# Contrast adjustment on one core: rows of 48 KB in four buffers instead of rows of 32 KB in six

## The chip, the core and the metric

The kernel runs on one core of a Trainium2 chip (trn2). The metric is the device time in microseconds (us). Single runs are compared by their median. Where kernels are compared, a ratio is given: the mean time of one kernel's fast runs over that of the kernel before in the same rounds on the same chip, with a 95% interval. It is therefore not quite the ratio of the medians quoted beside it. The profile measures a span that is some 2 us shorter than the device time (237.3 for a run of 239.14).

## The reference

The input is 16 x 3 images of 512 x 512 floats, 50.3 MB. Each image is pulled away from its own mean and clipped:

```python
def reference(x, factor):                       # factor = 1.5
    mean = np.mean(x, axis=(2, 3), keepdims=True)
    return np.clip(mean + factor * (x - mean), 0, 1).astype(np.float32)
```

So each pixel is read once and written once, 100.7 MB in all, and an image's output needs its whole sum first: `clip(factor * x + (1 - factor) * mean)`.

## The kernel before

A tile is 128 rows of 8192 floats (32 KB a row, 4 MB), which is four whole images of 32 rows each. Twelve tiles go through a ring of six buffers and are changed in place. The vector engine (DVE) and the scalar engine (ACT) each sum a part of the row. Two matmuls with a block matrix of ones times `(1-factor)/n_pix` add up the rows of an image and leave the shift on each row. DVE scales, shifts and clips, and ACT's queue stores.

```python
P, ROW, BUFS, SHORT = 128, 8192, 6, 2048
FIRST = (SHORT, ROW - SHORT)          # tile 0 is stored in two pieces
SUM = 4352
# ... pools, block matrix
def compute(t):
    xt = ring[:, t % BUFS, :]
    own = sums[:, 2 * t : 2 * t + 2]
    nc.vector.tensor_reduce(out=own[:, 0:1], in_=xt[:, 0:SUM], ...)
    nc.scalar.activation(out=junk, in_=xt[:, SUM:ROW], func=Act.Copy, accum_out=own[:, 1:2])
    shift = bias[:, t : t + 1]
    nc.tensor.matmul(shift, blockw, own[:, 1:2], start=True, stop=False)
    nc.tensor.matmul(shift, blockw, own[:, 0:1], start=False, stop=True)
    # ... DVE: part = part * factor + shift; part = min(max(part, 0), 1)
    # ... store, on ACT's DMA queue
with tc.manual_schedule():
    load(0, c1=SHORT)
    load(0, c0=SHORT)
    load(1)
    load(2, n=2)                      # one DMA loads two tiles
    load(4, n=2)
    for t in range(n_tiles):
        compute(t)
        if t + BUFS < n_tiles:
            load(t + BUFS)            # waits until the store of tile t has landed
```

## Time and profile before

| | before |
|---|---|
| device time, median of 4 runs | 239.24 us (238.97 to 239.35) |
| span of the profiled run | 237.3 us |
| DMA, share of sixteen engines' span (loads + stores) | 49.7% + 49.2% |
| DVE busy, ACT busy | 69%, 18% |
| DMAs (loads + stores) | 11 + 13 |

The DMA engines are the resource to watch: they are busy all the time while DVE has a third of its time free. The prediction below shows the lines and how they are read.

### The profile page before, as it was taken

What the parts mean: (1) busy time and instruction counts of PE and PEld (TensorE: products, weight loads), DVE (VectorE), ACT (ScalarE), POOL (GpSimd) and SP (SyncE); (2) the same over time, 40 slices, a digit from 0 to 9 for tenths busy, and PEclk for the clock granted to TensorE, in tenths of its full rate; (3) what the DMA queues carried; (4) which work ended last, traced back from release to release, by engine and by line L of the source; (5) the groups of instructions that cost most, each with busy time, mean ns of one, the idle gap of its engine ahead of it and who ended that gap; (6) DMA issues with size and microseconds to landing.
All of it is one profiled execution on the core that took longest, in us unless ns stands there. A gap on an engine that the chain in (4) does not pass through costs nothing.

```text
span 237.3 us, 285 instructions
## 1 busy us (share of the span) xinstructions
PE 14.1 (6%) x48; PEld 12.0 (5%) x48; DVE 163.1 (69%) x38; ACT 43.2 (18%) x25; POOL 0.9 (0%) x9
## 2 busy tenths in 40 slices
PE   0010010001010001010010100100100100010000
PEld 0010010001010001010010100100100100010000
DVE  0079989048989328999989898891892795687000
ACT  2050230041050023050320504101400500500000
POOL 1000000000000000000000000000000000000000
DMA  7999999999999999999999999999999999999996
GB/s 297 410 442 442 421 442 359 456 439 441 442 436 414 403 431 442 442 442 442 436 442 436 414 409 425 442 442 442 442 436 442 436 420 403 425 442 442 442 442 265
DMA packets 3712, 100.66 MB, mean 424 GB/s; under 512 B 384, under 2 KB 384, under 8 KB 384
## 3 DMA queue, kind: packets, MB, share of 16 engines
q1 hardware_dynamic: 1840, 50.33, 49.7%
q10 hardware_dynamic: 1872, 50.33, 49.2%
HBM read 50.33 MB, written 50.33 MB: 424 GB/s over the span
## 4 chain that ended last, share of the span: by engine, by line
DMA 57%; DVE 29%; another core or an unknown queue 3%; PE 1%; SPq 1%; issue 0%; DVEq 0%
DMA ring<-in_x_dram 41%; DMA out_dram<-ring 16%; DVE sums L81 10%; DVE ring L91 9%; DVE ring L94 9%; PE bias L87 1%; SPq L76 1%; DVEq L91 0%
## 5 line engine op out<-in xcount | busy, mean ns | idle before, releaser
L81 DVE TENSOR_REDUCE sums<-ring 128x1 f32<-128x4352 f32 x12 | 56.2, 4683 | 45.7 <-DMA ring<-in_x_dram 45.7
L84 ACT ACTIVATE junk<-ring 128x3840 f32<-128x3840 f32 x12 | 40.8, 3403 | 163.3 <-DMA ring<-in_x_dram 107.5
L91 DVE TENSOR_SCALAR ring<-ring,bias 128x8192 f32<-128x8192 f32 (+2 forms) x13 | 54.1, 4163 | 8.9 <-PE bias L87 7.4
L94 DVE TENSOR_SCALAR ring<-ring 128x8192 f32<-128x8192 f32 (+2 forms) x13 | 53.3, 4099 | 0.4
L86 PE MATMUL bias<-sums,blockw 128*128 128x1 f32 x24 | 7.0, 361 | 190.8 <-ACT junk L84 190.8
L86 PEld LDWEIGHTS bias<-sums,blockw 128*128 128x128 f32 x24 | 6.0, 312 | 191.7 <-ACT junk L84 175.2
L87 PE MATMUL bias<-sums,blockw 128*128 128x1 f32 x24 | 7.0, 363 | 4.3 <-DVE sums L81 3.9
L87 PEld LDWEIGHTS bias<-sums,blockw 128*128 128x128 f32 x24 | 6.0, 311 | 5.3 <-DVE sums L81 5.0
L84 ACT ACTIVATION_READ_ACCUMULATOR junk<-ring 128x1 f32 x12 | 2.2, 186 | 0.0
L84 ACT ACT_TABLE_LOAD x1 | 1.3, 1283 | 0.7 <-PEq L129 0.7
L63 POOL MEMSET blockw<- 32x32 f32 x4 | 0.5, 117 | 0.2
L61 POOL MEMSET blockw<- 128x128 f32 x1 | 0.2, 204 | 0.3 <-POOLq L129 0.3
L129 POOL MEMSET const-bfloat16-1.0<- 128x1 bf16 x1 | 0.1, 111 | 0.0
L129 POOL MEMSET const-uint8-127<- 128x1 uint8 x1 | 0.1, 111 | 0.0
L129 POOL MEMSET const-float32-1.0<- 128x1 f32 x1 | 0.1, 108 | 0.0
L129 POOL MEMSET const-float32-0.0<- 128x1 f32 x1 | 0.1, 103 | 0.2 <-issue 0.2
## 6 DMA issues: line engine op xcount, KB each, us to landing
out_dram<-ring ACTq DMA_DIRECT2D x11, 4096.0 KB, 35.8
ring<-in_x_dram SPq DMA_DIRECT2D x7, 4096.0 KB, 49.7
ring<-in_x_dram SPq DMA_DIRECT2D x2, 8192.0 KB, 66.7
ring<-in_x_dram SPq DMA_DIRECT2D x1, 3072.0 KB, 11.7
out_dram<-ring ACTq DMA_DIRECT2D x1, 3072.0 KB, 28.2
ring<-in_x_dram SPq DMA_DIRECT2D x1, 1024.0 KB, 4.8
out_dram<-ring ACTq DMA_DIRECT2D x1, 1024.0 KB, 17.5
```

The source lines that it names most:

```text
L61: nc.gpsimd.memset(blockw, 0.0)
L63: nc.gpsimd.memset(blockw[a : a + ppi, a : a + ppi], wconst)
L76: nc.sync.dma_start(out=ring[:, b : b + n, c0:c1], in_=src)
L81: nc.vector.tensor_reduce(out=own[:, 0:1], in_=xt[:, 0:SUM], axis=mybir.AxisListType.X, op=Alu.add)
L84: nc.scalar.activation(out=junk, in_=xt[:, SUM:ROW], func=Act.Copy, accum_out=own[:, 1:2])
L86: nc.tensor.matmul(shift, blockw, own[:, 1:2], start=True, stop=False)
L87: nc.tensor.matmul(shift, blockw, own[:, 0:1], start=False, stop=True)
L91: nc.vector.tensor_scalar(out=part, in0=part, scalar1=factor, scalar2=shift, op0=Alu.mult, op1=Alu.add)
L94: nc.vector.tensor_scalar(out=part, in0=part, scalar1=0.0, scalar2=1.0, op0=Alu.max, op1=Alu.min)
L129: nc = _bacc.Bacc("TRN2", target_bir_lowering=False, num_devices=1)
```

## The change

The intent is fewer and longer transfers: rows of 48 KB, so that six images fill a tile of 6 MB and eight tiles do; sixteen DMAs in place of 24. A row of 12288 floats is three thirds of 4096, and an image is 64 thirds, so some rows hold parts of two images. Each row therefore gets five partial sums, which the GpSimd engine multiplies with class masks; one matmul gives totals for all classes, and DVE picks one shift for each third. ACT scales one or two thirds, DVE the rest and the clip. Cut to its core:

```diff
-ROW = 8192
-BUFS = 6
-SHORT = 2048
-FIRST = (SHORT, ROW - SHORT)
-SUM = 4352
+PART = 4096
+ROW = 3 * PART
+HALF = PART // 2
+BUFS = 4
+FIRST = (HALF, ROW - HALF)
+HEAD = (ROW,)
 ... masks and block matrix built on GpSimd
     def compute(t):
+        nc.vector.tensor_reduce(out=own[:, 0:3], in_=xt[:, 0 : 3 * HALF] as 3 x 2048, ...)
+        for m, a, b in (3, 3 * HALF, 4 * HALF), (4, 2 * PART, ROW):
+            nc.scalar.activation(out=part, in_=part, func=Act.Copy, accum_out=own[:, m : m + 1])
+        pool.tensor_tensor(out=spread[:, t, :], in0=own (broadcast), in1=cls, op=Alu.mult)
+        nc.tensor.matmul(totals[:, t, :], blockw, spread[:, t, :], start=True, stop=True)
+        nc.vector.tensor_tensor(out=picked[:, t], in0=totals (broadcast), in1=pick, op=Alu.mult)
+        nc.vector.tensor_reduce(out=bias[:, t, :], in_=picked[:, t], axis=X, op=Alu.add)
+        kd = 1 if 0 < t < n_tiles - 1 else 2
+        for k in range(kd, 3):          # ACT scales thirds kd..2, DVE those before
+            nc.scalar.activation(out=third, in_=third, func=Act.Identity, scale=factor,
+                                 bias=bias[:, t, k : k + 1])
 ... DVE clips the row, store
-        load(0, c1=SHORT)
-        load(0, c0=SHORT)
+        for n in HEAD: load(0, c, c + n)
         load(1)
         load(2, n=2)
-        load(4, n=2)
```

More of the change, by code (lines that the diff above doesn't have):

```diff
@@ L10 @@
 P = 128
-ROW = 8192
-BUFS = 6
-SHORT = 2048
-FIRST = (SHORT, ROW - SHORT)
-SUM = 4352
+PART = 4096
[4 more added lines that the diff above has]
+HEAD = (ROW,)
+IMGS = 6
+CLS = 3
+NSUM = 5
 @with_exitstack
@@ L32 @@
     Act = mybir.ActivationFunctionType
+    X = mybir.AxisListType.X
     B, C, H, W = x.shape
     n_img, n_pix = B * C, H * W
-    ppi = n_pix // ROW
-    per_tile = P // ppi
-    n_tiles = n_img // per_tile
-    assert ppi * ROW == n_pix and per_tile * n_tiles == n_img
+    n_tiles = n_img // IMGS
+    assert IMGS * n_pix == P * ROW and IMGS * n_tiles == n_img and n_pix % PART == 0
+    units = n_pix // PART
     factor = float(factor)
@@ L45 @@
     out_f = out.rearrange("b c h w -> (b c h w)")
-    def dram(ap, t, c0=0, c1=ROW):
-        return bass.AP(tensor=ap.tensor, offset=t * P * ROW + c0, ap=[[ROW, P], [1, c1 - c0]])
     consts = ctx.enter_context(tc.tile_pool(name="consts", bufs=1))
@@ L53 @@
     psum = ctx.enter_context(tc.tile_pool(name="psum", bufs=1, space=bass.MemoryType.PSUM))
-    sums = small.tile([P, 2 * n_tiles], f32, name="sums")
-    junk = small.tile([P, ROW - SUM], f32, name="junk")
-    bias = psum.tile([P, n_tiles], f32, name="bias")
-    blockw = consts.tile([P, P], f32, name="blockw")
-    nc.gpsimd.memset(blockw, 0.0)
-    for a in range(0, P, ppi):
-        nc.gpsimd.memset(blockw[a : a + ppi, a : a + ppi], wconst)
+    sums = small.tile([P, n_tiles, NSUM], f32, name="sums")
@@ new lines @@
+    spread = small.tile([P, n_tiles, CLS * NSUM], f32, name="spread")
+    picked = small.tile([P, n_tiles, 3, CLS * NSUM], f32, name="picked")
+    bias = small.tile([P, n_tiles, 3], f32, name="bias")
+    totals = psum.tile([P, n_tiles, CLS * NSUM], f32, name="totals")
+    pool = nc.gpsimd
+    of = consts.tile([P, IMGS, NSUM], f32, name="of")
+    pool.memset(of, 1.0)
+    step = [[-2 * units, IMGS], [1, NSUM]]
+    pool.affine_select(
+        out=of, in_=of, pattern=step, compare_op=Alu.is_ge, fill=0.0, base=0, channel_multiplier=6
+    )
@@ new lines @@
+    pool.affine_select(
+        out=of, in_=of, pattern=[[2 * units, IMGS], [-1, NSUM]], compare_op=Alu.is_gt, fill=0.0,
+        base=2 * units, channel_multiplier=-6,
+    )
+    cls = consts.tile([P, CLS, NSUM], f32, name="cls")
+    pool.tensor_tensor(out=cls, in0=of[:, 0:CLS], in1=of[:, CLS:IMGS], op=Alu.add)
+    pick = consts.tile([P, 3, CLS, NSUM], f32, name="pick")
+    for k in range(3):
+        pool.tensor_copy(
+            out=pick[:, k], in_=cls[:, :, 2 * k : 2 * k + 1].to_broadcast([P, CLS, NSUM])
+        )
@@ new lines @@
+    blockw = consts.tile([P, P], f32, name="blockw")
+    pool.memset(blockw, wconst)
+    period = CLS * units // 3
+    p0 = 0
+    while p0 < period:
+        first, last = 3 * p0 // units, (3 * p0 + 2) // units
+        p1 = p0 + 1
+        while p1 < period and (3 * p1 // units, (3 * p1 + 2) // units) == (first, last):
+            p1 += 1
+        cols = blockw.rearrange("q (h p) -> q h p", p=period)[:, :, p0:p1]
+        pool.affine_select(
+            out=cols, in_=cols, pattern=[[-3 * period, P // period], [0, p1 - p0]],
+            compare_op=Alu.is_ge, fill=0.0, base=2 - units * first, channel_multiplier=3,
+        )
+        pool.affine_select(
+            out=cols, in_=cols, pattern=[[3 * period, P // period], [0, p1 - p0]],
+            compare_op=Alu.is_gt, fill=0.0, base=units * (last + 1), channel_multiplier=-3,
+        )
+        p0 = p1
@@ L66, with dram @@
     ring = xpool.tile([P, BUFS, ROW], f32, name="ring")
-    def load(t, c0=0, c1=ROW, n=1):
-        b = t % BUFS
-        src = bass.AP(
-            tensor=x_f.tensor,
+    def dram(ap, t, c0, c1, n=1):
+        return bass.AP(
+            tensor=ap.tensor,
             offset=t * P * ROW + c0,
@@ L75, in load, with store @@
         )
-        nc.sync.dma_start(out=ring[:, b : b + n, c0:c1], in_=src)
+    def load(t, c0=0, c1=ROW, n=1):
+        b = t % BUFS
+        nc.sync.dma_start(out=ring[:, b : b + n, c0:c1], in_=dram(x_f, t, c0, c1, n))
+    def store(t, c0, c1):
+        b = t % BUFS
+        nc.scalar.dma_start(out=dram(out_f, t, c0, c1), in_=ring[:, b : b + 1, c0:c1])
     def compute(t):
         xt = ring[:, t % BUFS, :]
-        own = sums[:, 2 * t : 2 * t + 2]
+        own = sums[:, t, :]
         nc.vector.tensor_reduce(
-            out=own[:, 0:1], in_=xt[:, 0:SUM], axis=mybir.AxisListType.X, op=Alu.add
-        )
@@ L84, in compute @@
-        nc.scalar.activation(out=junk, in_=xt[:, SUM:ROW], func=Act.Copy, accum_out=own[:, 1:2])
-        shift = bias[:, t : t + 1]
-        nc.tensor.matmul(shift, blockw, own[:, 1:2], start=True, stop=False)
-        nc.tensor.matmul(shift, blockw, own[:, 0:1], start=False, stop=True)
+            out=own[:, 0:3], in_=xt[:, 0 : 3 * HALF].rearrange("p (m c) -> p m c", m=3), axis=X,
+            op=Alu.add,
+        )
+        for m, a, b in (3, 3 * HALF, 4 * HALF), (4, 2 * PART, ROW):
+            part = xt[:, a:b]
+            nc.scalar.activation(out=part, in_=part, func=Act.Copy, accum_out=own[:, m : m + 1])
@@ new lines, in compute @@
+        pool.tensor_tensor(
+            out=spread[:, t, :].rearrange("p (r m) -> p r m", r=CLS),
+            in0=own[:, None, :].to_broadcast([P, CLS, NSUM]),
+            in1=cls,
+            op=Alu.mult,
+        )
+        nc.tensor.matmul(totals[:, t, :], blockw, spread[:, t, :], start=True, stop=True)
+        nc.vector.tensor_tensor(
+            out=picked[:, t],
+            in0=totals[:, t, :][:, None, :].to_broadcast([P, 3, CLS * NSUM]),
+            in1=pick.rearrange("p k r m -> p k (r m)"),
+            op=Alu.mult,
+        )
@@ L88, in compute @@
+        nc.vector.tensor_reduce(out=bias[:, t, :], in_=picked[:, t], axis=X, op=Alu.add)
+        kd = 1 if 0 < t < n_tiles - 1 else 2
+        for k in range(kd, 3):
+            third = xt[:, k * PART : (k + 1) * PART]
+            nc.scalar.activation(
+                out=third, in_=third, func=Act.Identity, scale=factor, bias=bias[:, t, k : k + 1]
+            )
         c = 0
         for n in FIRST if t == 0 else [ROW]:
-            part = xt[:, c : c + n]
-            nc.vector.tensor_scalar(
-                out=part, in0=part, scalar1=factor, scalar2=shift, op0=Alu.mult, op1=Alu.add
-            )
+            end = c + n
+            for k in range(kd):
+                a, b = max(c, k * PART), min(end, (k + 1) * PART)
+                if a < b:
+                    part = xt[:, a:b]
+                    nc.vector.tensor_scalar(
+                        out=part, in0=part, scalar1=factor, scalar2=bias[:, t, k : k + 1],
+                        op0=Alu.mult, op1=Alu.add,
+                    )
+            part = xt[:, c:end]
@@ L96, in compute @@
             )
-            store(t, c, c + n)
-            c += n
-    def store(t, c0, c1):
-        nc.scalar.dma_start(out=dram(out_f, t, c0, c1), in_=ring[:, t % BUFS, c0:c1])
-    with tc.manual_schedule():
-        load(0, c1=SHORT)
-        load(0, c0=SHORT)
+            store(t, c, end)
+            c = end
+    with tc.manual_schedule():
+        c = 0
+        for n in HEAD:
+            load(0, c, c + n)
+            c += n
         load(1)
         load(2, n=2)
-        load(4, n=2)
         for t in range(n_tiles):
```

## The prediction

> **What bounds the kernel now.** I read the page's row of 40 slices first, then the DMA view of chosen stretches, then the timeline and the groups by shape. The DMA row asks whether the sixteen DMA engines ever rest:
>
> ```profile
> DMA  7999999999999999999999999999999999999996
> ```
>
> Only the first and last slice (5.9 us each) are below nine tenths. The DMA view of the stretch from 2 to 235 us says it exactly:
>
> ```profile
> DMA packets 3688, 100.60 MB, mean 432 GB/s; under 512 B 368, under 2 KB 368, under 8 KB 368
> q1 hardware_dynamic: 1832, 50.27, 50.4%
> q10 hardware_dynamic: 1856, 50.33, 50.1%
> ```
>
> q1 is the load queue, q10 the store queue. Together their packets take 100.5% of the sixteen engines' time: there is no hole to fill. So the time is first byte (1.75 us), packets, and the end. What a packet costs comes from the same view of two stretches. From 60 to 180 us every data packet is a row of 32 KB:
>
> ```profile
> DMA packets 1769, 52.20 MB, mean 435 GB/s; under 512 B 176, under 2 KB 176, under 8 KB 176
> q1 hardware_dynamic: 889, 26.51, 51.1%
> q10 hardware_dynamic: 880, 25.69, 49.6%
> ```
>
> Taking off the 176 tiny ones (semaphores), 1593 packets take 100.7% of 16 x 120 us = 1933 us, so 1.213 us each. From 26 to 34 us the first tile's short store (8 KB rows) runs beside a load:
>
> ```profile
> q1 hardware_dynamic: 82, 2.69, 78.3%
> q10 hardware_dynamic: 81, 0.66, 19.6%
> ```
>
> 81 packets in 19.6% of 128 us: 0.310 us each. The difference, 0.903 us for 24 KB, is 0.301 us per 8 KB, so a packet is about 0.009 us fixed plus 0.301 us per 8 KB. By this line 24 KB takes 0.912, 40 KB 1.514 and 48 KB 1.815 us. These are estimates.
>
> The chain of waits could mislead here:
>
> ```profile
> 116.30 37.73 DMA out_dram<-ring
> ...
> 154.17 49.57 DMA ring<-in_x_dram
> ...
> 203.76 4.70 DVE sums L81
> ```
>
> It puts 29% of the span on VectorE (DVE), yet while those DVE pieces ran the queues were full. What the compute may not do is leave the queues empty. In the timeline the reductions that start a tile (start, duration, then the wait before):
>
> ```profile
> 165.03 4.69 DVE L81 TENSOR_REDUCE sums<-ring 128x1 f32<-128x4352 f32 x1 [4.99 <-DMA ring<-in_x_dram]
> 184.40 4.68 DVE L81 TENSOR_REDUCE sums<-ring 128x1 f32<-128x4352 f32 x1 [4.99 <-DMA ring<-in_x_dram]
> 203.76 4.69 DVE L81 TENSOR_REDUCE sums<-ring 128x1 f32<-128x4352 f32 x1 [4.98 <-DMA ring<-in_x_dram]
> ```
>
> They come 19.37 us apart. A tile has 8 rows per DMA engine, so a load and a store side by side are 16 packets x 1.213 = 19.4 us. DVE waits 5 us of each such period for data. The unit costs of compute come from the groups by shape (busy us, mean ns):
>
> ```profile
> L81 DVE TENSOR_REDUCE sums<-ring 128x1 f32<-128x4352 f32 x12 | 56.2, 4683 | 45.7 <-DMA ring<-in_x_dram 45.7
> L94 DVE TENSOR_SCALAR ring<-ring 128x8192 f32<-128x8192 f32 x11 | 48.7, 4427 | 0.4
> L84 ACT ACTIVATE junk<-ring 128x3840 f32<-128x3840 f32 x12 | 40.8, 3403 | 163.3 <-DMA ring<-in_x_dram 107.5 <-DVE ring L94 55.8
> L91 DVE TENSOR_SCALAR ring<-ring,bias 128x6144 f32<-128x6144 f32 x1 | 3.4, 3418 | 0.0
> ```
>
> **What the Trainium skill says.** (1) "DMA: Bandwidth & Descriptors", section "Queues, rings and completion order": each DMA engine takes turns between the queues that have work, a whole packet at a time. The trace agrees: 82 load against 81 store packets between 26 and 34 us, though a load packet is three to four times as long. (2) "VectorE: DVE Perf Modes", "The perf-mode tier table": fp32 tensor_scalar runs at twice the rate of tensor_reduce. The trace agrees: 4683 ns for 4352 elements (4533 at 0.96 GHz plus 150) against 4427 for 8192 (4267 at two per cycle plus 160). (3) "ScalarE: Activation LUTs", "What ACT_TABLE_LOAD costs": 186 ns plus 0.833 ns per element, and about 93 ns more for each per-partition pointer operand. The trace has 3403 for 3840 elements, so 204 plus 3199; the pointer form isn't in it. (4) "GPSIMD Engine Reference", "Elementwise — side-by-side cycle accounting": 4497 ns for a two-input tensor_tensor of 2048 elements. No two-input GpSimd operation is in this trace; its memsets take 103 to 204 ns.
>
> **The change, part by part.**
>
> *Longer rows, fewer DMAs.* Before, per DMA engine: 16 packets of 8 KB, 16 of 24 KB and 176 of 32 KB, 4.96 + 14.59 + 213.49 = 233.0 us. After: the first store's 8 of 8 KB and 8 of 40 KB, then 56 + 64 rows of 48 KB, 2.48 + 12.11 + 217.80 = 232.4 us. That is 0.65 us less. Eight semaphore packets fewer at some 0.009 us are 0.07 us. The bytes stay.
>
> *The single first DMA.* The first packet leaves at the same 1.75 us. Tile 0 is complete only after 8 x 1.815 us, at about 16.3, and compute starts near 17.2 instead of 12.9. That costs nothing by itself: the loads of tiles 0 to 3 are queued at once and are 32 packets x 1.815 = 58 us of work for each DMA engine even without stores.
>
> *The new compute per tile.* The longest of DVE's sum, 6144/0.96 + 150 = 6.55 us, and ScalarE's (ACT) two, 204 + 1707 and 204 + 3413 with two accumulator reads of 186, 5.9 us. Then GpSimd's product of 15 numbers (estimate 0.2), the matmul pair (0.6 in the chain before), two tiny DVE operations (0.2 each, nearly all fixed cost) and four hand-overs of some 0.08: 1.55 us. Then ACT scales two thirds, 2 x (204 + 3413 + 93) less some overlap, 7.4 us with hand-over, beside DVE's one third of 4096 (2.36 us); DVE then clips 12288, 6400 + 160 = 6.56 us. Sum 22.1 us per tile. Next tile's sums start only then. The last tile gives DVE two thirds (4.7 us) and is 19.4 us.
>
> *Does the chain keep the queues full?* A load and a store of 48 KB rows side by side last 16 x 1.815 = 29.0 us, above 22.1. I walked the two queues packet by packet with these durations, about 0.4 us from last packet to consumer and 2.2 us from issue to first packet. The same walk on the kernel before gives a span of 236.8 where the trace has 237.3, and its loads land within about 1 us. For the changed kernel: tile 0 done at 37, tile 1 at 59, the double load lands at 75 (it shares the DMA engines with stores), tiles 2 to 6 done at 98, 120, 142, 164 and 186, the last load lands near 191, and the last store is issued at 211.6. Store 6 keeps the engines busy until 220. So no hole appears, with 6 us to spare at the end.
>
> *Sum.* 239.24 - 0.65 - 0.07 = 238.5 us, 0.3% less. I say 238.6, since I trust fixed packet costs more than the rest.
>
> **The rivals.** *Compute becomes the bound.* From the double load's landing, five tiles of 22.1 us run almost without pause on DVE and ACT in turn; ACT's in-order queue holds the next sums behind the store's issue. For it: three engines hand over inside one chain, and the GpSimd operation is unmeasured. Against it: DVE and ACT unit costs are from this trace. In the walk, 2 us more per tile changes nothing, 4 us more open a hole of 7 us before the last store and give 246 us, twice the ACT thirds 265. It needs more than 2.6 us of error in a sum where only about 0.5 is unmeasured. *Four big buffers starve the loads.* A load waits until a whole 6 MB store has landed, where before it was 4 MB and six buffers. That would show as a DMA hole near 105 to 135 us; the walk has the loads of tiles 4 to 7 queued 28 us before they land. If 2 us were lost at each of four re-uses, 246 us. *Longer packets are slower or faster per byte.* The fixed part could be larger than read off (a row split in two descriptors costs nothing much, 128 x 0.009 = 1.2 us). Then 239 to 240. *The gain is larger:* impossible beyond the first and last 2 us, since the bytes at the present rate already fill the span.
>
> **Range and chances.** The packet sum fixes the floor near 238; the small uncertainties are some tenths each way, with a tail above from the chain of compute: 237.6 to 240.3. Faster by over 2% would need 234.5, under the packet sum plus both ends: 1%. Slower by over 2% needs a hole of 5 us: 5%. Within 2%: 94%.
>
> **What would show it right or wrong.** In the profile after: DMA shares of the two queues that add up to about 100% between 2 and 235 us; 48 KB packets of 1.81 us; reductions in the steady part 22 us apart at first, DVE idle in each tile while ACT scales its thirds; the double load landing near 75; the last store issued near 211 to 214. Wrong if the DMA row shows slices under 9 anywhere but at the ends, most likely around 205 to 225 us, if a tile takes over 24.5 us on the compute engines, or if a 48 KB packet takes more than 1.82 us.

## The result, and the profile after

The changed kernel takes 241.82 us, the median of four runs (241.38 to 242.36), against 239.24 before. The ratio is 1.0111 (1.0083 to 1.0138). Two later sets of runs gave 1.0072 and 1.0113. It is a loss of about 1%, within the 2% that was given a chance of 94%, but outside the range of 237.6 to 240.3 and on the other side of the time before. The profiled run has a span of 239.3 us, so 2.0 us more than before.

The page's DMA row of 40 slices after:

```profile
DMA  7999999999999999999999999999999999999993
```

No slice between the ends fell under nine tenths, as predicted. The DMA view from 2 to 235 us shows the shares, and the same view from 60 to 180 us a part of the steady run:

```profile
q1 hardware_dynamic: 1124, 49.74, 50.0%
q10 hardware_dynamic: 1278, 50.23, 49.8%
...
DMA packets 1205, 52.20 MB, mean 435 GB/s; under 512 B 128, under 2 KB 128, under 8 KB 128
q10 hardware_dynamic: 633, 27.23, 52.4%
q1 hardware_dynamic: 572, 24.97, 48.3%
```

The DMA engines were as busy as before (99.8% against 100.5%). These views count a packet in the stretch in which it begins, so the bytes of a stretch are right only to about one packet for each engine (0.8 MB with rows of 48 KB). From 60 to 180 us both kernels moved 52.20 MB: in the steady part longer rows gained nothing that this view can show. The chain of waits runs over DVE and ACT for most of the first 121 us, then over a store, a load from 162.44 us and the last tile's sum. The last load was there for compute at 198.66 us, 7 us later than the walk had it (near 191). The reductions that start a tile, from the timeline:

```profile
121.22 6.54 DVE L129 TENSOR_REDUCE sums<-ring 128x3 f32<-128x6144 f32 x1
143.16 6.55 DVE L129 TENSOR_REDUCE sums<-ring 128x3 f32<-128x6144 f32 x1
169.67 6.55 DVE L129 TENSOR_REDUCE sums<-ring 128x3 f32<-128x6144 f32 x1 [4.46 <-DMA ring<-in_x_dram]
198.66 6.55 DVE L129 TENSOR_REDUCE sums<-ring 128x3 f32<-128x6144 f32 x1 [6.93 <-DMA ring<-in_x_dram]
```

While compute runs without a wait, tiles are 21.94 us apart; later they are 29.0 us apart and DVE waits for loads. The groups by shape (busy us, mean ns, then the idle time before):

```profile
L129 DVE TENSOR_REDUCE sums<-ring 128x3 f32<-128x6144 f32 x8 | 52.4, 6549 | 47.1 <-DMA ring<-in_x_dram 47.1
L155 ACT ACTIVATE ring<-ring,bias 128x4096 f32<-128x4096 f32 x14 | 51.3, 3702 | 18.3 <-DVE bias L149 18.3
L170 DVE TENSOR_SCALAR ring<-ring 128x12288 f32<-128x12288 f32 x7 | 45.9, 6560 | 30.4 <-ACT ring L155 30.3
L136 POOL TENSOR_TENSOR spread<-sums,cls 128x15 f32<-128x15 f32 x8 | 1.7, 212 | 199.9 <-DVE sums L129 199.9
```

The predicted costs were 6.55, 3.71, 6.56 and 0.2 us. Compute is as predicted; the loss is elsewhere.

**Where the 2.0 us are.** The view by stretches (stretch, its length, busy time of each engine, then clock, DMA share and GB/s) gives for the kernel before

```profile
46.00:56.00 10.00, 1.17 (x4) 1.00 (x4) 4.69 (x1) 3.50 (x2) 0.00 (x0) 1.00 1.00 433
...
110.00:190.00 80.00, 5.87 (x20) 5.01 (x20) 65.33 (x16) 17.48 (x10) 0.00 (x0) 1.00 1.00 433
```

and for the changed one

```profile
46.00:56.00 10.00, 0.00 (x0) 0.00 (x0) 4.92 (x3) 7.31 (x2) 0.00 (x0) 1.00 1.00 409
...
110.00:190.00 80.00, 1.83 (x6) 1.51 (x6) 52.28 (x16) 43.44 (x20) 0.64 (x3) 1.00 1.00 433
```

The last column matters. The same view gave 430 against 430 from 1.7 to 20 us, 418 against 422 from 20 to 46, and 436 against 434 from 56 to 110. Summed over the stretches up to 190 us, before has moved 81.25 MB and after 81.01. That is 0.24 MB, or 0.55 us at 433 GB/s. The dip from 46 to 56 us is where the second piece of tile 0 (rows of 40 KB) begins to be stored beside a load. The DMA share is 1.00 there: the engines don't rest, their packets take longer.

So the sixteen engines together are some 0.6 us late. One engine is much later, and that comes out only at the very end. Each of the sixteen DMA engines closes a transfer with one tiny packet (the semaphore), so the tiny packets in the DMA view of the last microseconds count the engines that have finished. Before, from 235.4 to 235.9 us and after that:

```profile
DMA packets 14, 0.00 MB, mean 0 GB/s; under 512 B 14, under 2 KB 14, under 8 KB 14
...
DMA packets 2, 0.00 MB, mean 0 GB/s; under 512 B 2, under 2 KB 2, under 8 KB 2
```

After, from 235.4 to 236.5, from 236.5 to 237.5, and from 237.5 us on:

```profile
DMA packets 14, 0.05 MB, mean 45 GB/s; under 512 B 13, under 2 KB 13, under 8 KB 13
...
DMA packets 2, 0.00 MB, mean 0 GB/s; under 512 B 2, under 2 KB 2, under 8 KB 2
...
DMA packets 1, 0.00 MB, mean 0 GB/s; under 512 B 1, under 2 KB 1, under 8 KB 1
```

Before, all sixteen finish within 0.58 us, the last at 236.05. After, thirteen finish by 236.5, and one only at 238.17 us. The kernel ends with its slowest engine, since each engine moves its own sixteenth. The trace doesn't name the engine of a packet, but a packet begins 0.003 to 0.004 us before the one ahead of it on its engine ends. Strung together so, the packets of the changed kernel make sixteen chains of 6 MiB each (one has a packet of 8 KB too many, another one too few). The Trainium skill has this for loads, in a note that it marks as unconfirmed: a bulk load "runs at the pace of its slowest engine" ("DMA: Bandwidth & Descriptors", section "iDMA fabric"). Here the last stores show it.

**Which packets took longer.** The chains show where each engine loses its time: how far its packets run over their usual duration (1.213 us for 32 KB, 1.815 for 48 KB), summed by the time at which they begin, in us.

| packets that begin | before, mean engine | after, mean engine | after, slowest engine |
|---|---|---|---|
| up to 8 us | 0.45 | 0.85 | 1.60 |
| 8 to 46 us | 0.81 | 0.40 | 0.29 |
| 46 to 56 us | 0.00 | 0.59 | 0.52 |
| 56 to 110 us | 0.00 | 0.28 | 0.85 |
| from 110 us | 0.01 | 0.06 | 0.35 |
| sum | 1.27 | 2.19 | 3.61 |

The mean end of the sixteen engines moved from 235.68 to 236.27 us. That is the 0.92 us of longer packets and 0.07 us of idle time, less about 0.4 us for fewer packets. The slowest engine also idled for 0.52 us just before its long packet at 82.9 us. So its lag was made at a few packets long before the end, and not in the last stores.

In the changed kernel 119 of the 1920 packets of 48 KB ran over by more than 0.03 us, all but one of them loads, and most of the time lost lies where a queue begins: at the first packets of all, where the store queue goes to its next DMA near 50 us, and on four engines where the load queue starts again after it has run dry. The DMA views from 1.7 to 2.8, from 48 to 52 and from 82.8 to 83.3 us have

```profile
q1 hardware_dynamic: 16, 0.79, 240.4%
...
q1 hardware_dynamic: 32, 1.57, 104.8%
...
q1 hardware_dynamic: 4, 0.20, 122.2%
```

The first number counts load packets, and the last is their time as a share of sixteen engines' stretch: 2.64, 2.10 and 2.44 us for each packet, where 1.815 is usual. In the kernel before, too, long packets lie at the first packets and where the store queue begins or goes to its next DMA (23 to 28 and 35 to 41 us), and nearly none come later.

### The profile page after: what moved, and what is told of

It is laid out like the page before. It is cut to its first block, busy times and chain, and to the rows that moved or that the text cites. A ratio compares the mean times of both kernels' runs of the same rounds, so it can differ in the third digit from the quotient of the medians.

```text
span 239.3 us, 247 instructions
## 1 busy us (share of the span) xinstructions
PE 4.9 (2%) x16; PEld 4.0 (2%) x16; DVE 131.4 (55%) x44; ACT 97.4 (41%) x47; POOL 5.0 (2%) x30
## 4 chain that ended last, share of the span: by engine, by line
DMA 40%; DVE 32%; ACT 8%; another core or an unknown queue 7%; issue 2%; PE 1%; POOL 0%; POOLq 0%; ACTq 0%; DVEq 0%; SPq 0%
DMA ring<-in_x_dram 22%; DMA out_dram<-ring 17%; DVE ring L170 14%; DVE sums L129 14%; ACT ring L155 8%; DVE ring L165 4%; PE totals L142 1%; DVE picked L143 0%; DVE bias L149 0%; POOL spread L136 0%; POOLq L217 0%; POOLq L136 0%; ACTq L155 0%; DVEq L170 0%
## 5 line engine op out<-in xcount | busy, mean ns | idle before, releaser
L135 ACT ACTIVATE ring<-ring 128x2048 f32<-128x2048 f32 (+1 forms) x16 | 44.1, 2754 | 94.1 <-DMA ring<-in_x_dram 64.7
L129 DVE TENSOR_REDUCE sums<-ring 128x3 f32<-128x6144 f32 x8 | 52.4, 6549 | 47.1 <-DMA ring<-in_x_dram 47.1
L170 DVE TENSOR_SCALAR ring<-ring 128x12288 f32<-128x12288 f32 (+2 forms) x9 | 52.6, 5849 | 30.5 <-ACT ring L155 30.3
L155 ACT ACTIVATE ring<-ring,bias 128x4096 f32<-128x4096 f32 x14 | 51.3, 3702 | 18.3 <-DVE bias L149 18.3
L165 DVE TENSOR_SCALAR ring<-ring,bias 128x4096 f32<-128x4096 f32 (+1 forms) x11 | 23.6, 2158 | 0.3
L142 PE MATMUL totals<-spread,blockw 128*128 128x15 f32 x16 | 4.9, 384 | 201.4 <-POOL spread L136 201.4
L142 PEld LDWEIGHTS totals<-spread,blockw 128*128 128x128 f32 x16 | 4.0, 311 | 202.1 <-POOL spread L136 202.1
L136 POOL TENSOR_TENSOR spread<-sums,cls 128x15 f32<-128x15 f32 x8 | 1.7, 212 | 199.9 <-DVE sums L129 199.9
L135 ACT ACTIVATION_READ_ACCUMULATOR ring<-ring 128x1 f32 x16 | 3.0, 186 | 0.0
L97 POOL TENSOR_SCALAR_AFFINE_SELECT blockw<-blockw 128x42 f32<-128x42 f32 (+2 forms) x5 | 0.9, 219 | 0.0
L101 POOL TENSOR_SCALAR_AFFINE_SELECT blockw<-blockw 128x42 f32<-128x42 f32 (+2 forms) x5 | 0.9, 218 | 0.0
```

Source lines behind the costliest of these rows:

```text
L97: pool.affine_select(out=cols, in_=cols, pattern=[[-3 * period, P // period], [0, p1 - p0]], compare_op=Alu.is_ge, fill=0.0, base=2 - unit ...
L101: pool.affine_select(out=cols, in_=cols, pattern=[[3 * period, P // period], [0, p1 - p0]], compare_op=Alu.is_gt, fill=0.0, base=units * ( ...
L129: nc.vector.tensor_reduce(out=own[:, 0:3], in_=xt[:, 0 : 3 * HALF].rearrange("p (m c) -> p m c", m=3), axis=X, op=Alu.add,)
L135: nc.scalar.activation(out=part, in_=part, func=Act.Copy, accum_out=own[:, m : m + 1])
L136: pool.tensor_tensor(out=spread[:, t, :].rearrange("p (r m) -> p r m", r=CLS), in0=own[:, None, :].to_broadcast([P, CLS, NSUM]), in1=cls, ...
L142: nc.tensor.matmul(totals[:, t, :], blockw, spread[:, t, :], start=True, stop=True)
```

## The experiments

Four theories are named in the texts written before the runs. **S**: the start of a DMA queue costs each engine a lag of its own, and more so with long packets. **Q**: the load queue of the changed kernel runs dry near 77 us (its view shows 90.9% store packets from 76 to 82 us) and restarting it costs. **T**, formed after the first runs: the ring of four is too tight, so queues have no reserve. **C**: the chain of compute issues the last store late. All ran with five rounds.

The engine-end spread below is the time between the first and the last of the sixteen closing packets of the last store, in the run's trace.

### The changed kernel unaltered, as a control

No edit.

> The changed kernel unaltered, as a control on the same chip as the next three. Its first runs spread from 241.38 to 242.36 us while the kernel before spread only from 238.97 to 239.35. Theory S (every start of a DMA queue costs each of the sixteen DMA engines a lag of its own, larger with 48 KB packets, and the slowest engine sets the end): 241.4 to 242.4 again, a ratio of 1.009 to 1.013, with one or two engines still storing up to 2 us after the others have ended. Theory C (the compute chain issues the last store late): the same time, but a stretch before the last store in which the DMA share falls below 0.95. Chance of the machine: a ratio near 1.000.

It took 240.53 us (240.22 to 242.92), ratio 1.0072 (1.0043 to 1.0102). Its engines ended between 235.52 and 237.30 us, a spread of 1.78. The loss is real, and so is its unsteadiness: the kernel before ranged from 239.02 to 239.65 in the same rounds.

### The first load split again

```diff
-HEAD = (ROW,)
+HEAD = (HALF, ROW - HALF)
```

> Only the first load is split again, 8 KB of each row first, then 40 KB. Theory S: the first packets, 2.4 to 3.4 us instead of 1.81 in the changed kernel, were the start-up lag; with 8 KB first packets the lag of the median engine at 6 us falls by about 0.3 us and that of the worst by up to 0.9, so 0.3 to 1.0 us faster than the control. Theory Q (the load queue runs dry from 77 to 82 us and restarting it costs) and theory C: no change beyond 0.2 us.

242.07 us (239.45 to 243.66), ratio 1.0073 (1.0037 to 1.0110): inconclusive. (The run of 243.66 us is slow and is left out of the ratio.) The runs spread over 4 us, and in the profiled one a single engine ended at 239.19, 2.5 us after the next. An effect of half a microsecond cannot be seen here.

### The first tile stored whole

```diff
-FIRST = (HALF, ROW - HALF)
+FIRST = (ROW,)
```

> Only the first tile's store is one DMA instead of 8 KB and 40 KB rows. It then alternates one to one with the loads, is issued near 37 us and lands near 70, before the double load lands near 75; so the load of tile 4 is queued before the load queue runs dry. Theory Q: the restart lag (mean 0.4 us, worst engine 1.4) goes, 0.4 to 1.5 us faster than the control, and no stretch of store packets alone near 77 to 82 us. Theory S without Q: the start of the store queue still costs its lag once, 0 to 0.3 us faster. Theory C: the first tile's store starts later, no gain or up to 0.5 us slower.

248.21 us, ratio 1.0383 (1.0362 to 1.0403). All three theories missed. The load of tile 4 was indeed queued in time, but the whole store took half of the DMA engines' time from 42 us on, so the double load landed at 83.6 instead of 76.9 us. Tile 2 then started at 84.0 and not at 77.3, the last store was issued at 224.6 and not at 218.1 us, and by 110 us the rate had fallen (421 GB/s from 56 to 110 us, where the changed kernel has 434). So filling that one gap didn't help. As the edit moved everything after it, it doesn't refute theory Q: in the changed kernel's own profile the first load packets after the gap are long on four engines, the slowest one among them.

### Packets of half the length

```diff
+        for a in range(c0, c1, ROW // 2):
+            e = min(a + ROW // 2, c1)
+            nc.sync.dma_start(out=ring[:, b : b + n, a:e], in_=dram(x_f, t, a, e, n))
 ... the stores likewise
```

> Each load and store moves the same tile as two DMAs of 24 KB rows; buffers and compute stay. If the length of a packet is what costs (theory S), first packets and restarts lose half as much: 0.5 to 1.2 us faster than the control. If the packets' fixed part of about 9 ns mattered as I predicted, 128 more packets on each engine would make it 1.1 us slower. Theory Q and C: within 0.3 us of the control.

240.92 us (240.43 to 242.47), ratio 1.0074, so the same as the control. The engines ended within 1.03 us of each other, less unevenly than the control's 1.78. The median engine ended later (236.55 against 235.98), the last one earlier (236.95 against 237.30). So S's gain did not appear, and of the predicted loss of 1.1 us the median engine shows about half. It is not a clean test of the packets' length: the first halves of tiles 2 and 3 are now loaded before their second halves, so that tile 2 starts at 59.0 us (77.3 in the changed kernel) and tile 3 at 105.7 (99.3).

### The kernel before with one whole first load

```diff
-        load(0, c1=SHORT)
-        load(0, c0=SHORT)
+        load(0)
```

> The kernel before, with only its first tile's load made one DMA of 32 KB rows. Theory S (long first packets make the start slower and uneven between the sixteen DMA engines): 0.3 to 0.9 us slower than the kernel before. Theory T (below: the tight ring, not the start, costs): within 0.2 us.

239.75 us (239.73 to 240.23), ratio 1.0030 (1.0017 to 1.0043). The one DMA for the first tile costs 0.6 us by itself where the ring is deep. The prediction had said that it costs nothing. Only some 0.3 us of this lie in the profiled span (237.54 us in the mean of the runs, 237.27 before); there the first packets run over by 0.70 us for each engine instead of 0.45. The rest lies outside the span, where no trace shows a cause.

### The kernel before with four buffers

```diff
-BUFS = 6
+BUFS = 4
-        load(4, n=2)
```

> The kernel before, with four buffers of 32 KB rows instead of six; packets, compute and first load stay. Theory T: what the change lost is depth of the ring. With six buffers the next loads lie queued long before the load queue needs them; with four a load is issued only as the queue runs dry, and each restart of a queue lengthens packets on some engines, which then never catch up. So 1 to 4 us slower than before, with engines ending up to 2 us apart. Theory S (length of packets, single first load): no change, within 0.3 us.

240.12 us (239.56 to 241.40), ratio 1.0044 (1.0025 to 1.0062). The view by stretches, the kernel before first, then this run:

```profile
56.00:76.00 20.00, 1.18 (x5) 1.00 (x4) 19.07 (x5) 3.50 (x2) 0.00 (x0) 1.00 1.02 439
...
56.00:76.00 20.00, 1.18 (x4) 1.00 (x4) 19.18 (x5) 3.50 (x2) 0.00 (x0) 1.00 1.00 418
```

The DMA engines are as full and move 21 GB/s less for 20 us, which is 0.96 us at 439 GB/s: nearly the whole loss. (The view is coarse, as the share of 1.02 shows; by the packets' own durations, load packets that begin between 66 and 68 us run over by 0.70 us for each engine.) From 110 to 190 us both have 433. In this stretch one store has landed and the next begins (66 to 68 us) beside a load. The engines end within 0.42 us, so the part of theory T about uneven ends isn't borne out here; its loss of rate is.

### The kernel before with the first tile stored whole

```diff
-FIRST = (SHORT, ROW - SHORT)
+FIRST = (ROW,)
```

> The kernel before, with the first tile stored by one DMA. In the changed kernel this same edit cost some 8 us, by theory T since its ring of four leaves the queues no reserve. Theory T: with six buffers it costs nothing, within 0.4 us of before. If the edit itself were bad (a later first store): several us slower here too.

241.36 us (241.16 to 241.56), ratio 1.0092 (1.0079 to 1.0105). T had said no cost. Fifteen engines ended by 236.1 us, before's own time, and one at 237.75: a spread of 2.23 with rows of 32 KB and six buffers. So a single slow DMA engine can set the end with short rows too, and a deep ring doesn't prevent it.

### The changed kernel with a shorter chain of compute

```diff
-        kd = 1 if 0 < t < n_tiles - 1 else 2
+        kd = 2
```

> The changed kernel with VectorE scaling two thirds of every tile, not of the first and last alone; a tile's chain of compute is then about 19.4 us instead of 22. Theory C (the chain of compute is the bound): 2 us or more faster than the control's 240.5. Theory T: stores can be queued a little earlier but a load still waits for the store of four tiles before, which is DMA time: within 0.7 us of 240.5, run-to-run spread of 2 us as before.

240.85 us (240.61 to 242.19), ratio 1.0080 (1.0063 to 1.0097). Tiles that don't wait are now 19.3 us apart instead of 21.9, and the last store is issued at 218.5 (218.1 before that edit), since the last load sets it. Theory C falls: 2.6 us less compute for each tile bring nothing.

### Both edits in the kernel before

```diff
-BUFS = 6
+BUFS = 4
-        load(0, c1=SHORT)
-        load(0, c0=SHORT)
+        load(0)
-        load(4, n=2)
```

> The kernel before, with both edits that cost alone: the first load whole (alone 1.0030) and four buffers (alone 1.0044). Neither changes the rows of 32 KB nor the compute. If the change's loss is its start and its tight ring, and long rows add nothing, the two add up: 1.0074, 240.9 us, which is the changed kernel's 1.0072 to 1.0111. If long rows themselves cost, this stays under 1.005.

240.08 us (239.68 to 240.84), ratio 1.0042 (1.0029 to 1.0055). The two don't add up: beside four buffers the whole first load costs nothing more. The changed kernel is at 1.0072 to 1.0113, so the rest, 0.3 to 0.7 percent of the time, must come from what these two edits don't have. The load packets near 68 us run over by 0.34 us for each engine here, half of what they do with four buffers alone, so the whole first load has shifted the meeting of the queues that costs. With these edits the engines end evenly: the DMA view from 236 to 237 us has all sixteen closing packets.

### The kernel before with five buffers

```diff
-BUFS = 6
+BUFS = 5
-        load(4, n=2)
+        load(4)
```

> The kernel before with five buffers of 32 KB rows. Theory T: the cost of a tight ring sets in when the load queue runs dry before the next store has landed; with five buffers the queued loads are 21 MB and the first store lands near 52 us, before they are through near 70, so no restart: within 0.2% of before, 239.1 to 239.6. If every buffer less costs in proportion: half of the 1.0 us that four buffers cost.

239.38 us (239.37 to 239.49), ratio 1.0010 (0.9998 to 1.0022). The cost sets in between five and four buffers, not in proportion, as T had it.

### The loads of tiles 2 and 3 apart

```diff
-        load(2, n=2)
+        load(2)
+        load(3)
```

> The changed kernel with the loads of tiles 2 and 3 as two DMAs, so that tile 2 is computed from about 60 us on and not from 77, and its store is queued some 17 us earlier. Theory T: the load of tile 4 still waits for the first store, near 77 us, so the load queue still runs dry once; but the store queue keeps a reserve. 0 to 0.7 us faster than the changed kernel's 240.5 to 241.8. Theory C (late compute): 1 us faster or more and the last store issued well before 218 us.

243.46 us (243.14 to 246.55), ratio 1.0202 (1.0165 to 1.0239): 2% slower, where every theory had a gain or nothing. Tile 2 did start at 59.8 us. The view by stretches, of the changed kernel first, then of this run:

```profile
56.00:76.00 20.00, 0.00 (x0) 0.00 (x0) 4.11 (x1) 0.00 (x0) 0.00 (x0) 1.00 1.00 434
76.00:92.00 16.00, 0.61 (x2) 0.50 (x2) 9.32 (x4) 12.14 (x6) 0.22 (x1) 1.00 1.01 430
...
56.00:76.00 20.00, 0.61 (x2) 0.50 (x2) 13.82 (x6) 12.91 (x6) 0.22 (x1) 1.00 1.01 404
76.00:92.00 16.00, 0.61 (x2) 0.50 (x2) 14.87 (x5) 7.68 (x5) 0.21 (x1) 1.00 0.99 395
```

Again the engines are full, but the rate is 30 and 35 GB/s lower, which is 1.4 + 1.3 = 2.7 us. In the trace 67 of the first tile's 128 store packets of 40 KB take 1.8 to 1.9 us here, beside the load of tile 3, and all take 1.51 in the changed kernel. Near 84 us, where the load queue starts again after it has run dry, its first packet is long on all sixteen engines (by 0.8 us in the mean), not on four. From 92 us on the rate is 434 again. Why these packets take longer when the same bytes are asked for as two DMAs is open. I first suspected the compute that now runs beside them, but from 92 to 110 us the changed kernel has about as much of it, at 437 GB/s.

### That and the split first load

```diff
-HEAD = (ROW,)
+HEAD = (HALF, ROW - HALF)
-        load(2, n=2)
+        load(2)
+        load(3)
```

> The changed kernel with both: loads of tiles 2 and 3 apart, and the first load split in 8 KB and 40 KB of each row. If the start costs the changed kernel as it costs the kernel before (0.6 us for one whole first load), 0.6 us under the run with the loads apart; since the slowest of sixteen engines decides, the runs may spread over 2 us and hide it. No version of four 48 KB buffers should beat the kernel before (239.1).

243.67 us (242.93 to 243.78), ratio 1.0180 (1.0166 to 1.0193). The split first load gains nothing that the spread lets one see.

### The changed kernel once more

> The changed kernel a third time, for a third look at its sixteen DMA engines. So far its median engine ended at 236.0 us and its last one at 238.2 and 237.3; the median engine of the kernel before at 235.6 and the last at 236.1. If the slowest engine makes the loss: the span again follows the last engine by some 1.2 us, the median engine ends near 236, and the time lies between 240.2 and 242.9 us.

241.74 us (240.41 to 243.87), ratio 1.0113 (1.0073 to 1.0152). Thirteen engines ended by 236.3 us again, the last at 238.99. So three profiles of this kernel have last engines at 238.17, 237.30 and 238.99 us, and spans of 239.3, 238.5 and 240.2, each 1.1 to 1.2 us later. The span follows the slowest engine.

### The kernel before with packets of 16 KB

```diff
+        cuts = [c0] + [m for m in (ROW // 2,) if c0 < m < c1] + [c1]
+        for a, e in zip(cuts, cuts[1:]):
             ... one DMA for columns a to e, in load and in store
```

> The kernel before with every DMA of 32 KB rows cut in two DMAs of 16 KB rows: 176 more packets on each DMA engine. My prediction's 0.009 us of fixed cost per packet gives 1.6 us more, 240.7. The spacing of packets in the traces (1.2095 us for 32 KB, 1.8127 for 48 KB) leaves only some 0.004 to 0.005: 0.7 to 0.9 us more, 239.8 to 240.0. Engines' ends within 0.7 us of each other, as before.

251.64 us, ratio 1.0523 (1.0510 to 1.0535). This doesn't measure what it was meant to. The doubled stores blocked ACT's in-order queue. The timeline has two store issues as

```profile
115.95 6.12 ACTq L105 DMA_DIRECT2D out_dram<-ring  x2
```

Each took 0.34 us, but the second began only at 121.73 us. In the trace the program's DMAs use eight completion semaphores in turn, and an issue waits until the DMA that had its semaphore before has landed. With twice the DMAs these waits bite: the two stores came 0.4 us after loads that had landed at 115.53 and 121.31 us. ACT's next sum started only at 122.1 us, and compute fell so far behind that DMA slices near the end fell to two tenths. It does show one thing: from 130 to 190 us it moved 25.90 MB against 26.18 of the kernel before, 1.1% less, with twice the packets.

### The changed kernel with packets of 16 KB

```diff
+        for a in range(c0, c1, PART):
+            e = min(a + PART, c1)
+            ... one DMA for columns a to e; the stores are cut at PART and 2 * PART
```

> The changed kernel with each DMA cut into thirds, rows of 16 KB: some 250 more packets on each DMA engine than with 48 KB. If long packets are what drives the sixteen engines apart: ends within 1 us of each other (48 KB: 1.8 to 3.3, 24 KB: 1.1), while 0.0045 us for each packet add 1.1 us to all: 240.5 to 241.5, narrow spread of runs. If packets' length has no part in the unevenness: ends 2 us apart, 242 us.

246.41 us, ratio 1.0295 (1.0282 to 1.0308). Spoilt as well, by the same waits for semaphores: from 95 to 110 us it only loads, from 190 us on it only stores, and the store queue is empty for part of the time from 220 to 230 us. It decides nothing about the engines' unevenness.

### The kernel before with a first load of 2 KB rows

```diff
-        load(0, c1=SHORT)
-        load(0, c0=SHORT)
+        load(0, c1=512)
+        load(0, c0=512)
```

> The kernel before with 2 KB instead of 8 KB rows in the first load, an attempt at a version under both kernels. One whole first load cost 0.6 us; if shorter first packets go on helping the start, 0.1 to 0.3 us under before, 238.9; if the gain is exhausted at 8 KB, the same 239.1 to 239.3.

239.34 us (239.10 to 239.39), ratio 1.0006 (0.9993 to 1.0019): the same as before. No version beat the kernel before.

## Why the prediction was wrong

**Packets: right duration, wrong sum.** That "a packet is about 0.009 us fixed plus 0.301 us per 8 KB" held for durations: nearly all 48 KB packets in the trace take 1.815 us. But the step "0.65 us less" took durations for spacing. The prediction's own lines said 100.5% and 100.7%: packets of one engine overlap slightly, so only about half of the fixed part was on the path. Packets follow each other at 1.209 us (32 KB) and 1.812 us (48 KB), which leaves about 0.005 us fixed: an estimate of 0.35 us for 72 packets fewer on each engine, or 0.4 us with the semaphores, not 0.72.

**Compute: right.** The sum of 22.1 us per tile measured 21.94. "ScalarE: Activation LUTs" ("What ACT_TABLE_LOAD costs") held: ACT's scaling with a pointer operand took 3702 ns where its sum of as many elements took 3599, so 103 ns more (the page has 93). GpSimd's small product took 212 ns, as the prediction had estimated; it is too small to test the page's figure for 2048 elements. The double load landed for compute at 77.3 us (predicted near 75), the last at 198.7 (191), and the last store was issued at 218.05 (211.6), still before the store ahead of it ended at 221 to 224. The rival in which compute becomes the bound didn't happen: 2.6 us less per tile gained nothing.

**"So no hole appears": right, and not enough.** The rival "four big buffers starve the loads" was to show as a hole. It came as full DMA engines with slower packets. Four buffers alone cost the kernel before 0.4%, with the rate down to 418 GB/s in one stretch of 20 us, and five buffers cost nothing. In the changed kernel the stretches up to 190 us make 0.55 us.

**Of the single first DMA, "that costs nothing by itself": wrong.** Alone it cost 0.3% in the kernel before, but nothing on top of four buffers. In the changed kernel the packets up to 8 us run over by 0.85 us instead of 0.45, and those from 8 to 46 us by 0.40 instead of 0.81, so the mean engine has its loss back by then. The slowest engine has not: 1.60 us of its 3.61 are its first packet.

**The step that failed is the walk, "packet by packet with these durations".** It gave every packet one fixed duration, and one DMA engine stood for all sixteen; so no hole meant no loss, and the range had "some tenths each way". One of the prediction's own signs of being wrong, a 48 KB packet of more than 1.82 us, came true for 153 of 1920. Longer packets cost the mean engine 2.19 us where they had cost 1.27 before, and the slowest one 3.61 and 0.52 of idle time. The median engine lost about 0.4 us, its end moving from 235.63 to 236.07; the slowest lost 2.1 us, from 236.05 to 238.17, and it sets the end. In eight profiles with 48 KB packets (the unaltered kernel three times and five variants) the spread of ends went from 1.4 to 4.2 us; the run with 24 KB packets has 1.0, and the kernel before and its variants 0.4 to 0.7 with one exception of 2.2.

**What stays open.** That the unevenness goes with 48 KB packets is a tendency of these profiles and not shown: the run at 24 KB supports it (but has another order of loads), the one with the first store whole shows that 32 KB rows can have it too, and the runs with 16 KB were spoilt. The traces show that packets lengthen mostly where a queue begins; why they do, why other such places cost nothing, and why some engines lose more than others, no run here shows. Nor was any version found that takes the cost away.

## What to carry to other kernels

Here the DMA engines were full, and longer rows gained nothing in the steady part. Bigger tiles in fewer buffers take away the reserve that keeps both queues going: judge such a change by the depth of the ring in tiles, and read GB/s beside the DMA share, since full engines can still move less; then look for the packets that run over, which lie mostly where a queue begins. Add up a DMA-bound time from the spacing of packets, not from their durations, and leave room for the slowest of sixteen engines. Changes that move the order of loads and stores a little can cost several per cent, so try each by itself.

## What the Trainium skill lacked or had wrong

- "SBUF — State Buffer" ("The DMA setup-cost knee") advises to coalesce a DMA-bound transfer "into the largest single transfer you can". From 4 MB on it did not pay here: going from 24 DMAs to 16 and from 4 to 6 MB tiles gave 1.0072 to 1.0113 (with fewer buffers and another compute), and one DMA in place of two for the first tile alone 1.0030.
- No page that I read says that packets lengthen at full DMA share when queues start beside each other: 418 GB/s against 439 with four buffers, and 404 and 395 against 434 and 430 with two loads apart. Nor that the first packets of all do: 2.64 us each instead of 1.815.
- "DMA: Bandwidth & Descriptors" names the pace of the slowest engine only in passing, and for loads. Here it decided 2.1 us: 236.05 against 238.17.
- No page that I read says what it costs when a program's DMAs reuse completion semaphores: in the kernel before with packets of 16 KB, a store issue of 0.34 us began 5.4 us after the one before it had ended, 0.4 us after the load that had its semaphore had landed.
